# One output tensor with rows by partitions, nine unread products at the start, and an order for the first stage's splits in a hybrid encoder layer

## The chip, the cores and the metric

The kernel runs on one core of a Trainium2 chip. A core has a matrix engine (TensorE, PE in the profile, whose weight loads are shown apart as PEld), VectorE (DVE), ScalarE (ACT), GpSimd (POOL) and SyncE (SP), each with its own queue of instructions, and sixteen DMA engines that move data between main memory and the core. The metric is the device time of one execution in microseconds, lower is better; the time of a kernel is the median over its runs.

## The reference

One layer of a streaming encoder with two parallel mixers (a pooling mixer and a Mamba-2 scan, SSD) and a convolutional feed-forward block, for a prompt of 256 tokens and a sample of 32 tokens that share the weights. The width is 2048, the mixers have 1024 and 2048 channels, the feed-forward block 5632. Cut to what matters:

```
xn   = rmsnorm(x, norm_mix_pre)
proj = xn @ w_in                  # u | z | xBC | dt
y_pool, new_pool = pool_mixer(u, ...)
y_ssd, new_sconv, new_h = ssd_mixer(z, xbc, dt_raw, ...)
mix  = concat([y_pool, y_ssd]) @ w_out
x    = x + rmsnorm(mix, norm_mix_post)
hn   = rmsnorm(x, norm_ffn_pre)
up   = hn @ w_up
up, new_fconv = causal_dwconv(up, hist_fconv, ...)
f    = (silu(gate) * val) @ w_down
x    = x + rmsnorm(f, norm_ffn_post)
return x_prompt, x_sample, and the new states
```

All is float32. `rmsnorm` divides a token by the root of the mean of its squares over the 2048 channels.

## The kernel before

**Layout and products.** Channels lie on the 128 partitions, the 288 tokens (256 of the prompt, 32 of the sample) along the free axis, so x is sixteen tiles of 128 x 288, one for each k-step of a projection over 2048 channels. A float32 product is made of three products of a shorter format: each operand is split into a high part and a low part, and `mm3` (L135 to L138) adds weights-high by activations-high (L136), weights-high by activations-low (L137) and weights-low by activations-high (L138) in one PSUM accumulator. Plain float32 products occur too: the sum of squares (L242), the small projection for dt (L289) and some others.

**Weights.** They stream in through SP's queue into four buffers `raw`. ACT copies the high part, `whi` (L130, in the first stage L270), and DVE subtracts it from the original to get the low part, `wlo` (L131, L271), into four buffers each. A buffer comes free when TensorE has used it. In the same way ACT (L99) and DVE (L100) split the activations `xn`.

**The first stage** (L245 to L280) projects x onto six blocks of 128 columns (512 of the B and C inputs of the scan, 256 of its first channels): sixteen k-steps, 18 products each, in five accumulators `acc` and one `acc_x`. x is multiplied by the norm's gain but not yet by its reciprocal root: that, `rstd`, is applied when the accumulators are read out (L326, L327). Beside the splits, ACT squares the tiles of x (L230, L233; two buffers `xsq`), POOL adds the squares (L234), and at k = 13 `input_rstd` (L240) sums them over the channels by a product with `mean`, a tile filled with 1/2048 (`prs`, L242), followed by ACT's square root and DVE's reciprocal (L237, L238). After the stage come the products `pdt` (L289) and `pv` (L293) of the dt projection.

**The middle.** The projections of the mixers, the scan in groups of heads (decays `g`, masks `m`, products `py`), the output projection, the up projection and the down projection follow, each a call of `project`.

**The end.** Finished channel tiles are turned into rows of tokens by way of main memory (`fd`, `ft`). When the norm's factor of a row block is known, `y_out` (L963) multiplies and adds on DVE (L971) and writes 128 rows by 512 columns (256 KB) from SP's queue (L974). The second half of the prompt goes first, four writes; then the 32 sample rows, which lie as four blocks of 32 partitions (`xr_s`, 128 x 512), by one write (L1044); then the first half of the prompt, four writes.

**What sets the order.** Instructions are placed on each engine's queue by a scheduler from the program's order and priorities. `tc.keep_in_program_order` pins an instruction where the code has it, and `tc.issue_after(ins)` makes one stand behind another on the same engine. An engine works off its queue strictly from the front.

Of the kernel before, what the change touches and what calls it, by code (L numbers as in the profile page):

```python
# [8 lines left out]
F32 = mybir.dt.float32  # L9
F32R = mybir.dt.float32r  # L10
AF = mybir.ActivationFunctionType
# [5 lines left out]
P = 128  # L17
TC = {"schedule_with_timeline_sim": True}
D_MODEL = 2048
NP_ = 256  # L20
NS = 32
NT = NP_ + NS
D_POOL = 1024
D_SSD = 2048
# [6 lines left out]
NF = D_FF // P  # L31
NXC = CONV // P
NU = D_POOL // P
# [10 lines left out]
def body(  # L44
# [14 lines left out]
    w_up2,  # L59
    w_up,  # L60
    w_down,
    y_prompt,
    y_sample,
    new_pool,
    new_sconv,
    new_ssd_p,
# [4 lines left out]
    act, dve, pool, pe, sp = nc.scalar, nc.vector, nc.gpsimd, nc.tensor, nc.sync  # L71
# [11 lines left out]
    def aux(shape, name):  # L83
        return aux_ps.tile(shape, F32, tag="aux", name=name)

    def atile(name):
        return apool.tile([P, 2, NT], F32R, tag="a", name=name)
# [4 lines left out]
    def split_from(a, src, scale=None):  # L92

        if scale is None:
            act.activation(a[:, 0, :], src, AF.Copy)
            dve.tensor_tensor(a[:, 1, :], src, a[:, 0, :].bitcast(F32), op=ALU.subtract)
        else:
            return (
                act.activation(a[:, 0, :], src, AF.Copy, scale=scale),  # L99
                dve.scalar_tensor_tensor(  # L100
                    a[:, 1, :], src, scale, a[:, 0, :].bitcast(F32), op0=ALU.mult, op1=ALU.subtract
                ),
            )

    def wtile(part, n, nc_):

        t = wpool.tile([P, 1024 + 64], F32R, tag=part, name="w" + part)
        return t[:, 58 : 58 + n * nc_].rearrange("p (k c) -> p k c", k=n)
# [60 lines left out]
    def blocks_out(d, t, src, pool_):  # L169
# [12 lines left out]
    mean = const.tile([P, P], F32, name="mean")  # L182
# [4 lines left out]
        out=tri, in_=tri, pattern=[[1, P]], compare_op=ALU.is_ge, fill=0.0, base=0, channel_multiplier=-1  # L187
# [24 lines left out]
    g_mix_pre = const.tile([P, KD], F32, name="g0")  # L212
# [5 lines left out]
    start = ExitStack()  # L218
    xin = start.enter_context(tc.tile_pool(name="xin", bufs=1))
    xT = xin.tile([P, KD, NT], F32, name="xT")  # L220
# [4 lines left out]
    def input_tiles(kb, n):  # L225
        sp.dma_start(out=xT[:, kb : kb + n, :], in_=x_in[:, kb : kb + n, :])

    def input_squares(k):
        if k == 0:
            act.activation(xsum, xT[:, k, :], AF.Square)  # L230
        else:
            q = xin.tile([P, NT], F32, tag="xsq", bufs=2, name="xsq")
            act.activation(q, xT[:, k, :], AF.Square)  # L233
            pool.tensor_tensor(xsum, xsum, q, op=ALU.add)  # L234

# [4 lines left out]
    def input_rstd():  # L240
        p_ = aux([P, NT], "prs")
        pe.matmul(p_, mean, xsum, start=True, stop=True)  # L242
        root(rstd, p_)

    act.dma_start(out=g_mix_pre, in_=g0_in)  # L245
    input_tiles(0, 1)
    first = [acc_ps.tile([P, NT], F32, tag="acc", name="acc") if m < 5 else aux([P, NT], "acc_x") for m in range(6)]
    chunks = ((0, 1), (1, 1)) + tuple((k, 2) for k in range(2, KD, 2))
    x_with = {0: (1, 1), 1: (2, 2), 2: (4, 2), 4: (6, 3), 6: (9, 3), 8: (12, 4)}
    for kb, n in chunks:  # L250
        raw = wpool.tile([P, n, 768], F32, tag="raw", name="raw")
        sp.dma_start(out=raw, in_=w_first[:, kb : kb + n, :])
        if kb in x_with:
            input_tiles(*x_with[kb])
        if kb == 1:
            pool.dma_start(out=wdt, in_=w_dt)
        if kb == 2:
            pool.dma_start(out=par1, in_=par1_in)
            pool.dma_start(out=hp, in_=hp_in)
        if kb == 6:  # L260
            pool.dma_start(out=pc, in_=par2_in[:, :120])
            pool.dma_start(out=pf, in_=par2_in[:, 120:].rearrange("p (r t) -> p r t", r=6))
        for k in range(kb, kb + n):
            a = atile("xn")
            split_from(a, xT[:, k, :], g_mix_pre[:, k : k + 1])
            xn.append(a)
            hi, lo = wtile("hi", 1, 768)[:, 0, :], wtile("lo", 1, 768)[:, 0, :]
            step = 256 if k == 0 else 768
            for c in range(0, 768, step):
                act.activation(hi[:, c : c + step], raw[:, k - kb, c : c + step], AF.Copy)  # L270
                dve.tensor_tensor(  # L271
                    lo[:, c : c + step], raw[:, k - kb, c : c + step], hi[:, c : c + step].bitcast(F32), op=ALU.subtract
                )
            for t in range(k - 1, k) if 0 < k < 9 else range(2 * k - 10, 2 * k - 8) if 8 < k < 13 else ():
                input_squares(t)
            if k == 13:
                input_rstd()
            for m in range(6):
                c = slice(m * P, (m + 1) * P)
                mm3(first[m], hi[:, c], lo[:, c], a, k == 0, k == KD - 1)  # L280
# [5 lines left out]
    for r in range(4):  # L286
        for q in range(4):
            k = 4 * q + r
# [66 lines left out]
    def htile(name, n=NT, tag=None):  # L355
        return mp.tile([HEADS, n], F32, tag=tag or name, name=name, bufs={"z": 4}.get(tag, 2) if tag else 1)
# [22 lines left out]
    r = htile("r", tag="z")  # L379
# [196 lines left out]
    xT = op_.tile([P, KD, NT], F32, name="xT2")  # L576
# [66 lines left out]
    for t in range(NX):  # L643
        a = atile("mixs")
# [29 lines left out]
    for gi in range(2):  # L674
        c = slice(gi * P, (gi + 1) * P)
# [96 lines left out]
    for k in range(KD):  # L772
        if k % 2 == 0:
            raw = wpool.tile([P, 2, 896], F32, tag="raw", name="raw")
            with tc.high_priority(offset=ahead[0]):
                sp.dma_start(out=raw, in_=w_up1[:, k : k + 2, :])
        a = atile("hn")
        hi = act.activation(a[:, 0, :], x1[k], AF.Copy, scale=g_ffn_pre[:, k : k + 1])  # L778
# [8 lines left out]
        else:  # L787
            q = out_temp()
# [11 lines left out]
        for m in range(7):  # L800
            c = slice(m * P, (m + 1) * P)
# [32 lines left out]
    f = []  # L834
# [54 lines left out]
    for q in range(4):  # L889
        for b in range(2):  # L890
            t = apool.tile([P, 512], F32, tag="a", name="xr")
            sp.dma_start(out=t, in_=x1d[b * P : (b + 1) * P, 512 * q : 512 * (q + 1)])
            xr.append(t)
    xr_s = apool.tile([P, 512], F32, tag="a", name="xr_s")
# [68 lines left out]
    def y_out(q, b):  # L963

        x = xr[2 * q + b]
        f_ = ft[2 * q + b]
        for o, n, src in (
            ((0, 512, f_),) if q < 3 else ((0, 2 * P, f_[:, : 2 * P]), (2 * P, 2 * P, last[b]))
        ):
            c = slice(o, o + n)  # L970
            ins = dve.scalar_tensor_tensor(x[:, c], src, rf[:, b : b + 1], x[:, c], op0=ALU.mult, op1=ALU.add)  # L971
            if b:
                tc.keep_in_program_order(ins)
        sp.dma_start(out=y_prompt[0][b * P : (b + 1) * P, 512 * q : 512 * (q + 1)], in_=x)  # L974

    n_tok = [0]

# [20 lines left out]
    for kb, n in ((0, K_RUN), (K_RUN, 8), (K_RUN + 8, 8)):  # L998
        raw = fetch_w(wd2, kb, n, (KD - 2) * P, 256)
# [3 lines left out]
        for piece in split_w(raw, kb, n, 256):  # L1003
            for low in (True, False) if kb else (True,):
                for j in range(2):
                    c = slice(j * P, (j + 1) * P)
                    for k, hi, lo in piece:
                        a = f2[k]
# [8 lines left out]
    for j in range(2):  # L1017
        t = KD - 2 + j
# [4 lines left out]
    for j in range(2):  # L1023
        c = slice(j * P, (j + 1) * P)
# [16 lines left out]
    tc.keep_in_program_order(  # L1041
        dve.scalar_tensor_tensor(xr_s, ft_s, rf[:, 2:3], xr_s, op0=ALU.mult, op1=ALU.add)
    )
    sp.dma_start(out=y_sample[0].rearrange("s (q c) -> q s c", q=4), in_=xr_s)  # L1044
    p_f.append(acc_ps.tile([P, 4], F32, tag="acc", name="psum_f"))
    last[0] = acc_ps.tile([P, 2 * P], F32, tag="acc", name="pft")
    feature_sums(fsum, 1, True, False)
# [5 lines left out]
    for q in range(4):  # L1053
        y_out(q, 0)
# [1 line left out]


_OUTS = [
    (1, 256, 2048), (1, 32, 2048), (P, 2, 15, NU), (P, 2, 3, NXC), (P, D_SSD), (P, D_SSD), (P, 2, 2, 2 * NF),
]  # L1060


# [70 lines left out]
```

## Time and profile before

| | |
|---|---|
| median of 3 runs | 1330.14 us (1330.11 to 1331.14) |
| profiled execution | 1329.91 us |
| its span | 1328.2 us |
| TensorE busy | 1310.4 us (99%) |
| DVE, ACT, POOL busy | 884.6, 666.3, 215.0 us |
| moved by DMA | 249.81 MB, 188 GB/s on average |
| first product of the first stage | 5.71 us after the span's start |
| product `prs` (sum of squares) | 40.65 us |
| product `pdt` (after the first stage) | 48.32 us |
| last result row done by DVE | 1322.11 us |

The profile is one execution, recorded by the hardware. Its span is what lies between the first and the last instruction, and the execution took 1.71 us more. In a timeline a row has its start, its duration, the engine, the line and the operation with output and inputs; rows of one kind are folded (x3), and brackets hold the idle time of the engine ahead of it and what ended it. SPq rows are DMA issues. The matrix engine works in a pipeline, so that the duration of a product (0.3 us) is longer than the distance to the next (0.13 us).

### The profile page before, as it was taken

Reading aid. Unit: us, or ns where it says so; the run is one execution under the profiler, and the core shown is the slowest. Engines: PE = TensorE matmul, PEld = TensorE weight load, DVE = VectorE, ACT = ScalarE, POOL = GpSimd, SP = SyncE. Lnnn points to the kernel's source line nnn. Section 1 sums busy time; section 2 is a strip of 40 time slices with the busy share of each in tenths; the row PEclk is TensorE's granted clock in tenths of the full one; section 3 lists DMA queues with packets and bytes.
Section 4 is the critical chain, followed back from the end, with each engine's and each line's share of the span. In section 5 each row is a group of like instructions: output and inputs, shape, how many; then the busy total and the mean of one; then the engine's idle time right before and its main releaser. Section 6 shows DMA issues by size and latency. Waiting matters only on the chain.

```text
span 1328.2 us, 25077 instructions
## 1 busy us (share of the span) xinstructions
PE 1310.4 (99%) x10041; PEld 1295.1 (98%) x10041; DVE 884.6 (67%) x1460; ACT 666.3 (50%) x1002; POOL 215.0 (16%) x353
## 2 busy tenths in 40 slices
PE   7999999999999999999999999999999999999997
PEld 7999999999999989999999999999999999999996
DVE  8898998779644478977666643345666666664444
ACT  7558777446443455645445443334444444454442
POOL 6221102121211100211111100001111111101110
PEclk9999999999999999999999999999999999999998
DMA  7668884465666445666454454455444544566663
GB/s 287 230 194 255 287 242 160 140 240 206 232 206 207 147 143 195 199 188 185 164 183 162 151 175 161 160 180 177 172 159 164 186 159 159 175 235 175 209 181 93
DMA packets 104008, 249.81 MB, mean 188 GB/s; under 512 B 63748, under 2 KB 69444, under 8 KB 81492
## 3 DMA queue, kind: packets, MB, share of 16 engines
q1 hardware_dynamic: 101972, 243.11, 55.8%
q0 software_dynamic: 1488, 4.92, 1.1%
q8 instruction: 78, 1.28, 0.4%
q14 instruction: 38, 0.31, 0.1%
q10 hardware_dynamic: 432, 0.19, 0.1%
HBM read 236.23 MB, written 11.95 MB: 187 GB/s over the span
## 4 chain that ended last, share of the span: by engine, by line
PE 98%; DVE 1%; DMA 0%; ACT 0%; issue 0%; DVEq 0%; SPq 0%
PE acc L138 31%; PE acc L136 31%; PE acc L137 31%; PE acc_x L138 1%; PE acc_x L137 1%; PE acc_x L136 1%; PE py L467 1%; DVE xr L971 0%; PE run_a L1014 0%; PE low L1012 0%; DMA raw<-in_w_first 0%; PE py L469 0%; PE pst L701 0%; PE run_b L1027 0%; PE pdt L289 0%; DVE mg L764 0%
## 5 line engine op out<-in xcount | busy, mean ns | idle before, releaser
L131 DVE TENSOR_TENSOR wlo<-raw,whi 128x1024 fp32r<-128x1024 f32 (+1 forms) x386 | 464.0, 1203 | 334.7 <-ACT whi L130 332.5
L130 ACT ACTIVATE whi<-raw 128x1024 fp32r<-128x1024 f32 (+1 forms) x386 | 399.6, 1037 | 474.5 <-PE acc L137 382.9
L136 PE MATMUL acc<-hn,whi 128*128 128x288 f32 x1360 | 399.0, 294 | 0.1
L137 PE MATMUL acc<-hn,whi 128*128 128x288 f32 x1360 | 398.1, 293 | 0.0
L138 PE MATMUL acc<-hn,wlo 128*128 128x288 f32 x1360 | 397.7, 293 | 0.0
L136 PEld LDWEIGHTS acc<-hn,whi 128*128 128x128 f32 x1360 | 255.3, 188 | 0.9 <-ACT hn L778 0.9
L137 PEld LDWEIGHTS acc<-hn,whi 128*128 128x128 f32 x1360 | 255.3, 188 | 0.1
L138 PEld LDWEIGHTS acc<-hn,wlo 128*128 128x128 f32 x1360 | 255.2, 188 | 0.0
L136 PE MATMUL acc<-xn,whi 128*128 128x288 f32 x688 | 203.6, 297 | 5.7 <-ACT whi L270 5.7
L137 PE MATMUL acc<-xn,whi 128*128 128x288 f32 x688 | 200.6, 293 | 0.0
L138 PE MATMUL acc<-xn,wlo 128*128 128x288 f32 x688 | 198.6, 298 | 1.3 <-DVE wlo L271 1.3
L136 PE MATMUL acc<-fa,whi 128*128 128x288 f32 x660 | 194.0, 294 | 0.0
L137 PE MATMUL acc<-fa,whi 128*128 128x288 f32 x660 | 193.4, 293 | 0.0
L138 PE MATMUL acc<-fa,wlo 128*128 128x288 f32 x660 | 193.1, 293 | 0.0
L136 PEld LDWEIGHTS acc<-xn,whi 128*128 128x128 f32 x688 | 130.2, 189 | 6.6 <-ACT whi L270 5.7
L137 PEld LDWEIGHTS acc<-xn,whi 128*128 128x128 f32 x688 | 130.1, 189 | 0.2
L138 PEld LDWEIGHTS acc<-xn,wlo 128*128 128x128 f32 x688 | 127.8, 189 | 2.1 <-DVE wlo L271 1.5
L136 PEld LDWEIGHTS acc<-fa,whi 128*128 128x128 f32 x660 | 124.1, 188 | 0.0
L138 PEld LDWEIGHTS acc<-fa,wlo 128*128 128x128 f32 x660 | 123.9, 188 | 0.0
L137 PEld LDWEIGHTS acc<-fa,whi 128*128 128x128 f32 x660 | 123.9, 188 | 0.0
L825 POOL COPY fc_stage<-ebuf 128x4 f32<-128x4 f32 x88 | 27.2, 310 | 501.2 <-DVE ebuf L824 501.2
L831 DVE SCALAR_TENSOR_TENSOR fc<-ebuf,pf,fc 128x290 f32<-128x290 f32 x176 | 90.2, 518 | 2.9 <-ACT fc L829 0.3
(277 smaller groups left out, 1692.0 us busy)
## 6 DMA issues: line engine op xcount, KB each, us to landing
raw<-in_w_up SPq DMA_DIRECT2D x80, 1024.0 KB, 4.8
raw<-in_w_in SPq DMA_DIRECT2D x38, 1024.0 KB, 5.4
raw<-in_w_down SPq DMA_DIRECT2D x32, 1024.0 KB, 4.8
raw<-in_w_out SPq DMA_DIRECT2D x24, 1024.0 KB, 4.9
raw<-in_w_down SPq DMA_DIRECT2D x16, 768.0 KB, 4.3
raw<-in_w_up SPq DMA_DIRECT2D x8, 896.0 KB, 4.6
gb<-g_d SPq DMA_DIRECT2D x8, 832.0 KB, 6.4
raw<-in_w_first SPq DMA_DIRECT2D x7, 768.0 KB, 10.1
```

The lines of the kernel that those rows point to most:

```text
L130: act.activation(hi, raw[:, k : k + n, :], AF.Copy)
L131: dve.tensor_tensor(lo, raw[:, k : k + n, :], hi.bitcast(F32), op=ALU.subtract)
L136: pe.matmul(out, wh, a[:, 0, :], start=start, stop=False)
L137: pe.matmul(out, wh, a[:, 1, :], start=False, stop=False)
L138: pe.matmul(out, wl, a[:, 0, :], start=False, stop=stop)
L467: pe.matmul(y[:, 0:256], xw[:, 0, c], m[:, j, 0:256], start=True, stop=False)
L825: pool.tensor_copy(fc_stage[:, :, :, i], e[:, 256:324].rearrange("p (s c) -> p s c", c=34)[:, :, 0:2])
L831: dve.scalar_tensor_tensor(c, e[:, r_ : r_ + 290], pf[:, r_, i : i + 1], c, op0=ALU.mult, op1=ALU.add)
```

## The change

Three edits.

1. The two outputs `y_prompt` (1 x 256 x 2048) and `y_sample` (1 x 32 x 2048) become one, `y_rows` (128 x 9 x 512): for each partition eight pieces of prompt rows and one of sample rows. The host puts them back in shape.
2. Nine products of `mean` with itself, whose result `idle` nothing reads, stand at the front of TensorE's queue.
3. In the first stage the activation splits of step k stand behind the weight splits of step k - 2, and the squares behind the high split of step k - 1; squares have four buffers instead of two; `input_rstd` comes at k = 14 instead of 13.

```diff
-            q = xin.tile([P, NT], F32, tag="xsq", bufs=2, name="xsq")
+            q = xin.tile([P, NT], F32, tag="xsq", bufs=4, name="xsq")
...
+    cut = []
+    idle = aux([P, P], "idle")
+    for i in range(9):
+        tc.keep_in_program_order(pe.matmul(idle, mean, mean, start=True, stop=True))
...
             a = atile("xn")
-            split_from(a, xT[:, k, :], g_mix_pre[:, k : k + 1])
+            with ExitStack() as order:
+                for ins in cut[k - 2] if k > 2 else ():
+                    order.enter_context(tc.issue_after(ins.ins))
+                split_from(a, xT[:, k, :], g_mix_pre[:, k : k + 1])
...
-                act.activation(hi[:, c : c + step], raw[:, k - kb, c : c + step], AF.Copy)
-                dve.tensor_tensor(
+                w_hi = act.activation(hi[:, c : c + step], raw[:, k - kb, c : c + step], AF.Copy)
+                w_lo = dve.tensor_tensor(
...
+            cut.append((w_hi, w_lo))
             for t in range(k - 1, k) if 0 < k < 9 else range(2 * k - 10, 2 * k - 8) if 8 < k < 13 else ():
-                input_squares(t)
-            if k == 13:
+                with tc.issue_after(cut[k - 1][0].ins):
+                    input_squares(t)
+            if k == 14:
                 input_rstd()
...
-        sp.dma_start(out=y_prompt[0][b * P : (b + 1) * P, 512 * q : 512 * (q + 1)], in_=x)
+        sp.dma_start(out=y_rows[:, 4 * b + q, :], in_=x)
...
-    sp.dma_start(out=y_sample[0].rearrange("s (q c) -> q s c", q=4), in_=xr_s)
+    sp.dma_start(out=y_rows[:, 8, :], in_=xr_s)
...
 _OUTS = [
-    (1, 256, 2048), (1, 32, 2048), (P, 2, 15, NU), (P, 2, 3, NXC), (P, D_SSD), (P, D_SSD), (P, 2, 2, 2 * NF),
+    (P, 9, 512), (P, 2, 15, NU), (P, 2, 3, NXC), (P, D_SSD), (P, D_SSD), (P, 2, 2, 2 * NF),
 ]
...
+    y_p = _np.ascontiguousarray(y[:, :8].reshape(P, 2, D_MODEL).transpose(1, 0, 2)).reshape(1, NP_, D_MODEL)
+    y_s = _np.ascontiguousarray(y[:, 8].reshape(4, NS, 512).transpose(1, 0, 2)).reshape(1, NS, D_MODEL)
```

How the queues change is best seen in their order. First DVE in the first stage, from the third k-step on: `xn` are activation splits, `wlo` weight splits, `rstd` the reciprocal. Before:

```order
L100 SCALAR_TENSOR_TENSOR xn<-xT,g_125,xn 128x288 x2
L271 TENSOR_TENSOR wlo<-raw,whi 128x768 x2
L100 SCALAR_TENSOR_TENSOR xn<-xT,g_125,xn 128x288 x6
L271 TENSOR_TENSOR wlo<-raw,whi 128x768 x2
L100 SCALAR_TENSOR_TENSOR xn<-xT,g_125,xn 128x288 x4
L271 TENSOR_TENSOR wlo<-raw,whi 128x768 x8
L131 TENSOR_TENSOR wlo<-raw,whi 128x1024
L238 RECIPROCAL rstd<-rstd 128x288
```

Now, up to the same end (ahead of these rows, two activation splits and two weight splits alternate from k = 4 on):

```order
L99 SCALAR_TENSOR_TENSOR xn<-xT,g_125,xn 128x288 x2
L277 TENSOR_TENSOR wlo<-raw,whi 128x768 x2
L99 SCALAR_TENSOR_TENSOR xn<-xT,g_125,xn 128x288 x2
L277 TENSOR_TENSOR wlo<-raw,whi 128x768
L99 SCALAR_TENSOR_TENSOR xn<-xT,g_125,xn 128x288
L277 TENSOR_TENSOR wlo<-raw,whi 128x768
L99 SCALAR_TENSOR_TENSOR xn<-xT,g_125,xn 128x288
L277 TENSOR_TENSOR wlo<-raw,whi 128x768 x2
L130 TENSOR_TENSOR wlo<-raw,whi 128x1024 x2
L237 RECIPROCAL rstd<-rstd 128x288
```

Where six and then four activation splits stood together, none stands more than two ahead of a weight split. Two weight splits of the next projection, not one, stand ahead of the reciprocal.

TensorE at the start of its queue, now (before, it begins with the second of these rows; rows that repeat are left out):

```order
L249 MATMUL idle<-mean 128x128 x9
L135 MATMUL acc<-xn,whi 128x288
L136 MATMUL acc<-xn,whi 128x288
L137 MATMUL acc<-xn,wlo 128x288 x2
L135 MATMUL acc_x<-xn,whi 128x288
```

The product `prs` stands behind 252 products of the stage where it stood behind 234.

SP's queue around the decays `g`, whose rows go to main memory and come back as `gb`. Before:

```order
L175 DMA xs_d<-blocks 32x9x32
L392 DMA g_d<-g 32x416
L175 DMA xs_d<-blocks 32x9x32 x3
L437 DMA gb<-g_d 128x1664 x2
L441 DMA xw<-xs_d 128x2x256
```

Now:

```order
L400 DMA g_d<-g 32x416
L174 DMA xs_d<-blocks 32x9x32 x4
L445 DMA gb<-g_d 128x1664 x2
L449 DMA xw<-xs_d 128x2x256
L450 DMA xw<-xs_d 128x256
```

The write of g has moved ahead of the first of the four writes of `xs_d`. On DVE and ACT there are more small moves of this kind up to about 250 us of the program, mostly weight splits that stand one place earlier among the vector work. At the end of SP's queue only a form changes: the write of `xr_s` is `4x32x512` before and `128x512` now.

More of the change, by code (lines that the diff above doesn't have):

```diff
@@ L61, in body @@
     w_down,
-    y_prompt,
-    y_sample,
+    y_rows,
     new_pool,
@@ L1119 @@
     r = _run(nc, [arrays], core_ids=[0])
-    y_p, y_s, n_pool, n_sconv, h_p, h_s, n_fconv = (_np.asarray(r.results[0][f"out_{i}"]) for i in range(len(_OUTS)))
+    y, n_pool, n_sconv, h_p, h_s, n_fconv = (_np.asarray(r.results[0][f"out_{i}"]) for i in range(len(_OUTS)))
     def rows(a, s):
```

## The prediction

> **What bounds the kernel now.** I read the page first, then TensorE's waits, then the timeline of the two ends of the span, since a kernel whose TensorE hardly pauses can gain only where it does.
>
> ```profile
> span 1328.2 us, 25077 instructions
> PE 1310.4 (99%) x10041; PEld 1295.1 (98%) x10041; DVE 884.6 (67%) x1460; ACT 666.3 (50%) x1002; POOL 215.0 (16%) x353
> PE 98%; DVE 1%; DMA 0%; ACT 0%; issue 0%; DVEq 0%; SPq 0%
> PE acc L136 <- ACT whi L270: 5.7, 1, 5.7
> PE acc L138 <- DVE wlo L271: 1.3, 1, 1.3
> ```
>
> The first rows are the span and each engine's busy time, the third the chain of work that ended last, the last two are TensorE's longest waits (total, times, longest). The span is 1328.2 us, TensorE is busy for 1310.4 of it, and 98% of the chain runs on it. So the kernel is a queue of products, and there are four places to gain: the 5.7 us before the first product, products that run slowly, the one wait of 1.3 us, and what follows the last product. The change touches all of these. The profiled execution took 1329.91 us, 1.71 more than its span and 0.23 less than the median, 1330.14; I sum against 1329.91 and add the 0.23 at the end.
>
> **The nine products ahead.** The timeline of the start (start, duration, engine, line, operation, and in brackets what ended the idle time before):
>
> ```profile
> 0.95 0.20 POOL L183 MEMSET mean<- 128x128 f32 x1
> 5.71 0.61 PE L136 MATMUL acc<-xn,whi 128*128 128x288 f32 x1 [5.71 <-ACT whi L270]
> 6.36 0.44 PE L136 MATMUL acc<-xn,whi 128*128 128x288 f32 x1
> 6.60 0.44 PE L137 MATMUL acc<-xn,whi 128*128 128x288 f32 x1
> 10.42 1.58 ACT L270 ACTIVATE whi<-raw 128x768 fp32r<-128x768 f32 x2 [1.47 <-DMA raw<-in_w_first]
> 11.14 0.29 PE L137 MATMUL acc<-xn,whi 128*128 128x288 f32 x1
> 11.27 0.30 PE L136 MATMUL acc<-xn,whi 128*128 128x288 f32 x1
> 12.86 0.29 PE L136 MATMUL acc<-xn,whi 128*128 128x288 f32 x1
> ```
>
> Products start 0.24 us apart at 6.36 and 6.60 and 0.13 apart at 11.14 and 11.27: TensorE starts at about half its rate. The step lies between 10.7 and 10.9, 5.1 us after the first product. The clock column says 1.00 in this stretch, so the pitch is my evidence. These windows count what ran slowly:
>
> ```profile
> 5.71:10.80 5.09, 5.09 (x21) 5.09 (x22) 3.95 (x7) 3.62 (x9) 2.49 (x5) 1.00 1.01 375
> 10.80:12.86 2.06, 2.06 (x17) 2.06 (x16) 1.57 (x3) 2.00 (x4) 0.00 (x0) 1.00 1.03 416
> 12.86:48.32 35.46, 34.16 (x257) 33.66 (x255) 30.22 (x33) 23.67 (x44) 15.65 (x19) 1.00 0.74 279
> ```
>
> Twenty-one products at 0.24 cost 21 x 0.11 = 2.3 us more than fast ones. Not all can be had. The k-step that starts at 12.86 is the third one (k = 2); its weights are split by the ACT row at 10.42, whose two pieces take 0.79 each, so whi is there at 11.21, and that row itself waited for the transfer. Before that moment products of k = 2 cannot run at any clock. With a fast clock from the start, 36 products take 36 x 0.1325 = 4.8 us and end at 10.5; TensorE then waits for 11.21. So the third k-step starts near 11.25 instead of 12.86: **-1.6 us**.
>
> Are the nine done by 5.71? They read mean alone, written by 1.15. Their price comes from the one fp32 product of similar kind:
>
> ```profile
> 40.65 0.65 PE L242 MATMUL prs<-xsum,mean 128*128 128x288 f32 x2
> 40.81 0.48 PE prs L242 x2
> ```
>
> The first is the product's two records in the timeline, the second its share in the chain: 0.48 us for 288 columns, so 0.21 for 128, and about 0.43 at the slow pitch. Nine take 1.9 to 3.9 us and end between 3.2 and 5.2, ahead of 5.71. If the clock steps 5.1 us after the first of them, that is at 6.4. A step up to about 7.3 costs nothing (seven slow products lose 0.8 us, what lies between 10.5 and 11.25). The bounds: no effect on the clock, 0; step before 7.3, -1.6. I take the upper end, because in this trace steady products did release the clock after 5.1 us and the nine start 4.4 us earlier.
>
> The Trainium skill, TensorE: Matmul & The Clock Gate, Part 1: The HAM clock gate, says the rate is released after a busy window of about 3.4 us whose phase is free-running. By it the step would fall 3.4 to 6.8 us after the first of the nine, at 4.7 to 8.1, and the term would be -1.25 to -1.6; the trace's 5.1 us lies inside.
>
> **The order of the splits in the first stage.** DVE writes the low parts of activations (L100) and weights (L271) in one queue:
>
> ```profile
> 17.98 4.32 DVE L100 SCALAR_TENSOR_TENSOR xn<-xT,g,xn 128x288 fp32r<-128x288 f32 x6
> 25.19 3.53 DVE L100 SCALAR_TENSOR_TENSOR xn<-xT,g,xn 128x288 fp32r<-128x288 f32 x4
> 28.64 5.63 DVE L271 TENSOR_TENSOR wlo<-raw,whi 128x768 fp32r<-128x768 f32 x5
> 28.65 0.30 PE L137 MATMUL acc_x<-xn,whi 128*128 128x288 f32 x1
> 30.25 0.94 PE L138 MATMUL acc<-xn,wlo 128*128 128x288 f32 x5 [1.30 <-DVE wlo L271]
> ```
>
> Six and then four activation splits stand ahead of weight splits that TensorE needs sooner. Its product at 28.65 is followed at 30.25 instead of 28.78: 1.46 us lost from start to start (1.30 in the wait's own count). The new order has pairs: two activation splits, two weight splits. A pair of each costs 2 x 0.72 + 2 x 0.75 = 2.9 us on DVE against 4.8 us for two k-steps on TensorE (18 products of 0.1325 each), so DVE stays ahead. The transfers fill 0.74 of the stretch from 12.86 to 48.32 (the third window above), and no wait of TensorE in it is put down to one, so I take it that they land in time when needed 3 us earlier; ACT's splits stand in the same pairs. **-1.46 us**, bounds -1.3 and -1.46, and 0 if a piece is still late.
>
> A check: from 11.25, fourteen k-steps of 2.385 and the 0.48 of the sum of squares end at 45.1. Before, the product after them started here:
>
> ```profile
> 48.32 2.15 PE L289 MATMUL pdt<-xT,wdt 128*32 128x288 f32 x32
> 43.62 1.96 DVE L238 RECIPROCAL rstd<-rstd 128x288 f32<-128x288 f32 x1 [0.59 <-ACT rstd L237]
> ```
>
> That is 3.1 us earlier, as the two terms say.
>
> **The sum of squares one k-step later, four buffers for squares.** The reciprocal ended 45.58 - 40.65 = 4.9 us after its product began. Moved one k-step (2.4 us) later, it ends about 0.3 us before the stage's last product (36 products, 4.8 us, and its own 0.48 lie between), and the five accumulators are multiplied by it while TensorE does pdt (2.15 us). The group of the first evacuations by DVE:
>
> ```profile
> L326 DVE TENSOR_TENSOR ebuf<-acc,rstd 128x256 f32<-128x256 f32 x5 | 2.1, 419 | 0.3 <-POOL ebuf L319 0.3
> ```
>
> Behind the reciprocal stand one weight split (1.2 us), two of these (0.42 each) and a small rest (0.2, an estimate by its 32 columns), so the first accumulator is free about 1.9 us after the stage's end and needed 2.2 after it: a cover of 0.3. If it failed, TensorE would wait for DVE's next evacuations, up to 1 us. I take 0 and keep +1.
>
> **The output tensor.** The tail, on SP's queue and DVE:
>
> ```profile
> 1315.26 2.45 SPq L974 DMA_DIRECT2D out<-xr  x4
> 1318.62 0.70 SPq L1044 DMA_DIRECT2D out<-xr_s  x1
> 1320.02 4.14 SPq L974 DMA_DIRECT2D out<-xr  x4
> 1321.63 0.48 DVE L971 SCALAR_TENSOR_TENSOR xr<-pft,rf,xr 128x256 f32<-128x256 f32 x1
> DMA to landing us min/median/max: 2.0/2.1/2.1
> L974 SPq DMA_DIRECT2D out<-xr x2: 391/812/1233, 1322.4 to 1322.9; - x2
> DMA to landing us min/median/max: 4.2/4.2/4.3
> 1320.00:1321.00 1.00, 0.00 (x0) 0.00 (x0) 1.00 (x2) 0.00 (x0) 0.00 (x0) 1.00 0.32 25
> 1323.00:1324.00 1.00, 0.00 (x0) 0.00 (x0) 0.00 (x0) 0.00 (x0) 0.00 (x0) 0.50 0.93 350
> ```
>
> The four writes ahead of the sample's issue quickly and land 2.0 to 2.1 us after issue (first landing row). The four behind take 4.14 us to issue, and the last two, issued at 1322.4 and 1322.9, land 4.2 to 4.3 after. In between the queues move 25 GB/s, later 350 (last column): the sample write, which goes out as 4 x 32 x 512, trickles and holds those behind it. In the new kernel it is 128 x 512, the same form as its neighbours, so I give it and the last four the 2.1 us of the first four. DVE finishes the last xr at 1321.63 + 0.48 = 1322.11; its write lands at 1324.25 where the last one landed at 1322.9 + 4.3 = 1327.2. **-2.95 us**; bounds 0 (the trickle has another cause) and -3.0.
>
> The Trainium skill, DMA: Bandwidth & Descriptors, Why a DMA increments its semaphore by 16 and not by 1, says that a transfer runs on the largest number of engines up to 16 that divides the slowest dimension on both sides: 4 for the old form, 16 for the new. It would give the same term; the windows' 25 GB/s against 350 agree with it.
>
> One tensor fewer and the reshaping on the host lie outside the span's work: 0, since 1.71 us around the span show no room for more than a few tenths.
>
> **What moves afterwards.** Up to about 250 us DVE, ACT and SP run in a slightly different order, and everything starts 3 us earlier. TensorE waits nowhere there now, but the margins are thin:
>
> ```profile
> 129.78 1.89 DVE L460 TENSOR_TENSOR m<-m,cbt 128x1664 f32<-128x1664 f32 x1
> 131.76 0.65 PE L467 MATMUL py<-m,xw 128*64 128x256 f32 x4
> 178.50 1.22 DVE L131 TENSOR_TENSOR wlo<-raw,whi 128x1024 fp32r<-128x1024 f32 x1
> 180.07 0.29 PE L138 MATMUL acc<-xn,wlo 128*128 128x288 f32 x1
> ```
>
> The mask product is done at 131.67 and read at 131.76, 0.1 us later; a weight split is done at 179.72 and read at 180.07, 0.35 later. Were the vector work not to move earlier with TensorE, up to 3.0 us of the gain would come back as waits there. It should move: the splits between 50 and 95 us wait for TensorE's release of their buffers, the weight splits stand a place earlier in the new order, and the transfer of the decays (g) is issued sooner. I take +0.3, bounds 0 and +3.0.
>
> **Sum:** -1.6 - 1.46 - 2.95 + 0.3 = -5.71, or 1324.20 on the profiled execution, **1324.4 us** beside the median.
>
> **Rivals.** (a) The sample write was not what held the tail, for instance because DVE's late rows or the closing clock do. For it: the clock column stands at 0.50 in the last of those windows. Against it: DVE is done at 1322.11 and data flows for 4 us more. Only -2.76 remains: 1327.4. Chance 0.10. (b) Waits after 100 us take back the stage's gain, because SSD transfers rather than TensorE set the pace; for it speaks the 0.1 us margin: 1329.91 - 2.95 + 0.23 = 1327.2. Chance 0.10. (c) The clock is not released by unread products or comes late: without the -1.6, 1326.0. Chance 0.07. (d) Slower: the nine do not overlap their weight loads and run one record after the other at the slow rate. By the cold rows a record would be 0.33 load and 0.44 product, two records each, p = 1.54 a product. They end at 1.3 + 9p = 15.2; the weights have landed meanwhile, the stage then takes 38.7 us and ends at 53.9 instead of 48.3. Less the tail's 2.95 that is +2.65: 1332.8. It is slower than before from p = 1.25 on. Against it: in the trace a weight load runs while the product before it does:
>
> ```profile
> 5.88 0.33 PEld L137 LDWEIGHTS acc<-xn,whi 128*128 128x128 f32 x1
> ```
>
> It lies inside the product of 5.71 to 6.32. Chance 0.05. The Trainium skill speaks for (d): TensorE: Matmul & The Clock Gate, What overlaps and what doesn't, lets a weight load overlap only where the row groups differ, which here they don't; the row disagrees. (e) The change does not act: the unread products are not run, or two rivals fall together, (a) with (b) giving no change. Chance 0.06, half of it slower than before.
>
> **Numbers.** The forecast holds 0.62: its own range is 1323.5 (every term at its best, with 0.3 for the scatter of runs) to 1325.5. To leave out no more than 0.2 the range goes to 1327.4, which takes in (c), (b) and half of (a). About 0.2% (2.7 us, 1327.5 and 1332.8) is what a measurement here can tell from no change. Faster: 0.62 + 0.07 and most of (a) and (b), 0.82; same 0.10, from the far halves of (a) and (b) and part of (e); slower 0.08, from (d) and (e).
>
> **What would show it.** The clock: products 0.13 apart soon after 6.4, the third k-step at 11.25; 0.24 beyond 8 would speak for (c). The first real product still at 5.71; at 10 or later, (d). The 1.3 us row of TensorE's waits gone and pdt at 45.2; a new row on wlo, or on acc against DVE's evacuations, says which term failed. The last four writes issued in some 0.35 us each and landing 2.1 after; the span ending 2.2 to 3 us after DVE's last row rather than 6.1; otherwise (a). Waits of TensorE on m, ce or wlo between 100 and 210 us would be (b). Wrong in kind I would be if TensorE's busy time fell or grew by more than 3 us in a stretch that I have not named.

## The result: 1324.07 us, and the profile after

| | before | changed |
|---|---|---|
| median of 5 runs | 1330.12 us (1330.04 to 1331.14) | 1324.07 us (1323.57 to 1324.38) |
| ratio, with its 95% interval | | 0.9951 [0.9938, 0.9964] |
| profiled execution | 1329.91 us | 1323.83 us |
| its span | 1328.2 us | 1322.1 us |

The changed kernel is 6.05 us faster by the medians; the forecast was 1324.4. The page after, with the rows that answer to the first ones of before:

```profile
span 1322.1 us, 25117 instructions
PE 1312.0 (99%) x10059; PEld 1296.7 (98%) x10059; DVE 882.6 (67%) x1460; ACT 667.1 (50%) x1002; POOL 224.9 (17%) x353
```

TensorE's waits (total, times, longest), whole list:

```profile
PE idle L249 <- POOL mean L182: 1.2, 1, 1.2
PE acc L135 <- ACT whi L276: 1.2, 1, 1.2
PE psum_f L939 <- ACT fsq L968: 0.8, 1, 0.8
PE psum_m L753 <- ACT msq L676: 0.7, 1, 0.7
```

The wait on a low weight split is gone. In its place stands one of 1.2 us on a high split (ACT's), which was not there. The first row is no loss: it is what comes ahead of the nine products. The timeline shows where the second one lies:

```profile
1.21 4.04 PE L249 MATMUL idle<-mean 128*128 128x128 f32 x18 [1.21 <-POOL mean L182]
5.32 0.40 PE L135 MATMUL acc<-xn,whi 128*128 128x288 f32 x1
5.56 0.30 PE L136 MATMUL acc<-xn,whi 128*128 128x288 f32 x1
10.67 1.58 ACT L276 ACTIVATE whi<-raw 128x768 fp32r<-128x768 f32 x2 [1.25 <-DMA raw<-in_w_first]
11.57 0.40 PE L135 MATMUL acc<-xn,whi 128*128 128x288 f32 x1 [1.18 <-ACT whi L276]
45.65 2.15 PE L297 MATMUL pdt<-xT,wdt 128*32 128x288 f32 x32
```

The nine products (18 records) run from 1.21 to 5.25, done before the first real one. That one starts at 5.32 and the pitch is fast almost at once. But at 11.57, where the third k-step starts, TensorE has stood still for 1.18 us: ACT's split began at 10.67, when the transfer of these weights had landed. The product after the stage starts at 45.65 instead of 48.32.

The tail:

```profile
1315.61 0.33 SPq L1052 DMA_DIRECT2D out<-xr_s  x1
1317.01 2.45 SPq L982 DMA_DIRECT2D out<-xr  x4
1318.62 0.48 DVE L979 SCALAR_TENSOR_TENSOR xr<-pft,rf,xr 128x256 f32<-128x256 f32 x1
DMA to landing us min/median/max: 2.0/2.0/2.1
1319.00:1320.00 1.00, 0.00 (x0) 0.00 (x0) 0.10 (x1) 0.00 (x0) 0.00 (x0) 0.53 0.98 363
```

All eight writes of result rows land 2.0 to 2.1 us after issue (fourth row), the four behind the sample's write issue as fast as those ahead of it (2.45 us for four, 4.14 before), and in the microsecond from 1319 us on, in which DVE finishes its last row (1319.10), the queues already move 363 GB/s.

The account between the two profiled executions, by four marks:

| stretch | before | changed | difference | forecast |
|---|---|---|---|---|
| span's start to the third k-step | 12.86 | 11.57 | -1.29 | -1.6 |
| third k-step to `pdt` | 35.46 | 34.08 | -1.38 | -1.46 |
| `pdt` to DVE's last result row | 1273.79 | 1273.45 | -0.34 | +0.3 |
| that row to the span's end | 6.09 | 3.00 | -3.09 | -2.95 |
| sum | 1328.2 | 1322.1 | -6.1 | -5.71 |

The sizes stand close to the forecast's. Whether the causes are those of the forecast was the question of the experiments.

### The profile page after: what moved, and what is told of

Its sections match the earlier page's. It is cut to its first block, busy times and chain, and to the rows that moved or that the text cites. A ratio compares the mean times of both kernels' runs of the same rounds, so it can differ in the third digit from the quotient of the medians.

```text
span 1322.1 us, 25117 instructions
## 1 busy us (share of the span) xinstructions
PE 1312.0 (99%) x10059; PEld 1296.7 (98%) x10059; DVE 882.6 (67%) x1460; ACT 667.1 (50%) x1002; POOL 224.9 (17%) x353
## 4 chain that ended last, share of the span: by engine, by line
PE 98%; DVE 1%; DMA 1%; ACT 0%; SPq 0%; issue 0%; DVEq 0%
PE acc L135 31%; PE acc L137 31%; PE acc L136 31%; PE acc_x L137 1%; PE py L475 1%; PE acc_x L135 1%; PE acc_x L136 1%; DMA raw<-in_w_first 1%; DVE xr L979 0%; PE run_a L1022 0%; PE low L1020 0%; PE py L477 0%; PE pst L709 0%; PE run_b L1035 0%; PE pdt L297 0%; DVE mg L772 0%
## 5 line engine op out<-in xcount | busy, mean ns | idle before, releaser
L137 PE MATMUL acc<-xn,wlo 128*128 128x288 f32 x688 | 194.9, 295 | 0.0
L829 POOL COPY ebuf<-pf 128x2 f32<-128x2 f32 x88 | 71.2, 810 | 122.8 <-DVE fc L839 79.4
```

Source lines behind the costliest of these rows:

```text
L137: pe.matmul(out, wl, a[:, 0, :], start=False, stop=stop)
L829: pool.tensor_copy(e[:, 258:260], pf[:, 4:6, i])
```

## The experiments

In all of them the kernel before was run beside on the same chip; its medians lay between 1329.94 and 1330.49 us. The ratios are to it.

**One: the output tensor alone.** The edit to the kernel before, beside the host's reshaping:

```diff
-        sp.dma_start(out=y_prompt[0][b * P : (b + 1) * P, 512 * q : 512 * (q + 1)], in_=x)
+        sp.dma_start(out=y_rows[:, 4 * b + q, :], in_=x)
...
-    sp.dma_start(out=y_sample[0].rearrange("s (q c) -> q s c", q=4), in_=xr_s)
+    sp.dma_start(out=y_rows[:, 8, :], in_=xr_s)
```

> The kernel before with the one output tensor alone. My theory: the sample write in the form 128 x 512 no longer holds the four writes behind it, so the span ends about 3.0 us after DVE's last result row instead of 6.1, and nothing else moves: 1327.0 to 1327.2 us. Rival: the three gains of the change are not independent, and the tail gains only because the tail runs at another moment or clock: 1329 or more.

Measured: 1327.76 us, ratio 0.9979 [0.9970, 0.9988]. The profiled execution gave 1326.76. The gain is 2.7 us, and TensorE's wait of 1.3 us on the low split is still in its list. The median lies 0.6 us above the range expected, the profiled execution 0.2 below it; the span ends 3.07 us after DVE's last row, as expected. The tail is a term of its own.

**Two: the form without the one tensor.** Two output tensors, the sample's as 128 x 512:

```diff
-    sp.dma_start(out=y_sample[0].rearrange("s (q c) -> q s c", q=4), in_=xr_s)
+    sp.dma_start(out=y_sample, in_=xr_s)
...
-    (1, 256, 2048), (1, 32, 2048), ...
+    (1, 256, 2048), (P, 512), ...
```

> The kernel before with its two output tensors kept, but the sample's laid out as 128 x 512, so that its write goes out in that form. If the form of the one write is what held the tail, the last four writes land 2.1 us after issue and the gain is that of the one tensor, 2.7 to 3.1 us. If one tensor for all rows matters, the time stays that of the kernel before.

Measured: 1327.10 us, ratio 0.9978 [0.9969, 0.9986]. Issues of SP at the end, and the landing of the last four writes:

```profile
1318.59 0.33 SPq L1044 DMA_DIRECT2D out<-xr_s  x1
1319.99 2.45 SPq L974 DMA_DIRECT2D out<-xr  x4
DMA to landing us min/median/max: 2.0/2.1/2.2
```

The whole of the tail's gain is there with two tensors. It is the form of one write of 256 KB, not the number of tensors.

**Three: the nine products alone.**

```diff
+    idle = aux([P, P], "idle")
+    for i in range(9):
+        tc.keep_in_program_order(pe.matmul(idle, mean, mean, start=True, stop=True))
```

> The kernel before with the nine unread products alone. Theory A: DVE's queue in the first stage has no idle time from 11.3 to 34.3 us, so the weight split that TensorE waits for still ends at 30.2; the third k-step starts 1.3 us earlier, the wait at that split grows from 1.3 to about 2.6 us, and the time stays at 1330.1 (1329.8 to 1330.3). Theory B, as the sum of the prediction has it: the terms add, and the time is 1328.6 to 1328.9.

Measured: 1331.12 us, beside 1330.49 for the kernel before, ratio 1.0006 [0.9997, 1.0014]: nothing gained. That is 0.8 us above theory A's range, on the far side from theory B. TensorE in the first stage:

```profile
11.71 0.40 PE L136 MATMUL acc<-xn,whi 128*128 128x288 f32 x1 [1.13 <-ACT whi L273]
22.66 0.40 PE L136 MATMUL acc<-xn,whi 128*128 128x288 f32 x1 [1.11 <-ACT whi L273]
30.65 0.93 PE L138 MATMUL acc<-xn,wlo 128*128 128x288 f32 x5 [1.36 <-DVE wlo L274]
48.74 1.66 PE L292 MATMUL pdt<-xT,wdt 128*32 128x288 f32 x24
```

The third k-step starts 1.15 us earlier than in the kernel before (11.71 against 12.86), TensorE then waits 1.11 us more for a high split and again for the low one, and `pdt` comes no earlier (48.74 against 48.32). Theory A stands, with one difference: what was gained is lost at a second wait, not by a longer first one. That second wait is for ACT: its high split starts at 21.78, behind a square that stood 0.54 us waiting for POOL's sum. The terms of the forecast do not add.

**Four: the changed kernel without the nine products.**

```diff
-    idle = aux([P, P], "idle")
-    for i in range(9):
-        tc.keep_in_program_order(pe.matmul(idle, mean, mean, start=True, stop=True))
```

> The changed kernel without the nine unread products. The start falls back to the slow pitch, 0.24 us between products until about 10.8 us, and the third k-step to 12.9 us: 1.3 us more than the changed kernel, 1325.2 to 1325.5. If the clock rose for another reason than the nine products, it stays at 1324.1.

Measured: 1324.14 us (1323.86 to 1324.58), ratio 0.9953 [0.9940, 0.9965], against 1324.07 with them. The number is the one of the second expectation, but not for its reason: the slow pitch did come back, as the first had it, and the time did not.

```profile
5.34 0.61 PE L135 MATMUL acc<-xn,whi 128*128 128x288 f32 x1 [5.34 <-ACT whi L273]
5.98 0.44 PE L135 MATMUL acc<-xn,whi 128*128 128x288 f32 x1
6.22 0.44 PE L136 MATMUL acc<-xn,whi 128*128 128x288 f32 x1
...
8.86 0.59 PE L137 MATMUL acc<-xn,wlo 128*128 128x288 f32 x3
9.29 0.30 PE L137 MATMUL acc_x<-xn,wlo 128*128 128x288 f32 x1
9.43 0.29 PE L135 MATMUL acc<-xn,whi 128*128 128x288 f32 x1
...
11.81 0.30 PE L135 MATMUL acc<-xn,whi 128*128 128x288 f32 x1
...
45.68 2.15 PE L294 MATMUL pdt<-xT,wdt 128*32 128x288 f32 x32
```

Products are 0.24 us apart at 6 us, and the three from 8.86 to 9.29 take 0.14 each: here the fast pitch begins 3.5 us after the first product (8.86 against 5.34), not 5.1. Even with about 15 slow products the third k-step starts at 11.81, 0.24 later than with the nine, because with them TensorE waits there for the transfer. From there to `pdt` are 33.87 us, which is exactly fourteen k-steps of 2.385 and the 0.48 of `prs`: no wait.

**Five: the order alone**, without the nine products and with two output tensors:

```diff
-            split_from(a, xT[:, k, :], g_mix_pre[:, k : k + 1])
+            with ExitStack() as order:
+                for ins in cut[k - 2] if k > 2 else ():
+                    order.enter_context(tc.issue_after(ins.ins))
+                split_from(a, xT[:, k, :], g_mix_pre[:, k : k + 1])
...
-            q = xin.tile([P, NT], F32, tag="xsq", bufs=2, name="xsq")
+            q = xin.tile([P, NT], F32, tag="xsq", bufs=4, name="xsq")
...
-                input_squares(t)
-            if k == 13:
+                with tc.issue_after(cut[k - 1][0].ins):
+                    input_squares(t)
+            if k == 14:
```

> The kernel before with the order of the splits, the four buffers and the later sum of squares alone (no unread products, two output tensors). Both theories: the wait of 1.3 us on the weight split is gone and the first product after the stage starts at 46.9 instead of 48.3. The further 0.3 us at the second group of masked products (131.8 us) also goes if the order of DVE's queue made it, and stays if only the moment did: 1328.4 or 1328.7 us.

Measured: 1327.17 us, ratio 0.9975 [0.9966, 0.9985]. Both theories missed the time by more than a microsecond. `pdt` starts at 45.95, a microsecond earlier than they had it: the fast pitch began 4.0 us after the first product in this execution instead of 5.1, and the third k-step stands at 12.09 instead of 12.86. By the medians the order alone is worth 3.3 us (2.7 between the profiled executions); with the tail's 2.7 this makes 6.05, as much as the whole change gained. The second group of masked products starts 0.23 us after the product ahead of it (0.42 before); its mask is done 1.6 us ahead. In the kernel before, the group starts at 131.76, and this is the product ahead of it:

```profile
131.34 0.29 PE L138 MATMUL acc<-xn,wlo 128*128 128x288 f32 x1
```

In the profiles with the old order this distance is 0.42, 0.64, 0.22 and 0.23 (before, and experiments three, one and two): with the old order it differed from profile to profile. No profile with the whole new order shows the wait.

**Six and seven: the order in halves.** The first piece of that diff alone (the activation splits), and the other two alone (the squares, and `prs` one k-step later).

> The kernel before with the order of the activation splits alone (squares in two buffers and in their old places, sum of squares at k = 13). If the pairs on DVE's queue are what removed the wait, TensorE has no wait on a weight split and the first product after the stage stands at 45.9 to 46.8 as with the whole order: 1327.1 to 1328.4 us. If the squares' two buffers hold ACT, and by it DVE, part of the wait stays.

> The kernel before with the other half: four buffers and bound places for the squares, the sum of squares one k-step later, the activation splits in their old order. By the same reason the wait on the weight split stays at 1.3 us or near it and the time at that of the kernel before, 1329.6 to 1330.3 us. If ACT's waits for the squares were the cause, the wait goes.

Measured: 1328.41 us, ratio 0.9985 [0.9976, 0.9994], and 1327.41 us, ratio 0.9976 [0.9967, 0.9985]. The first has no wait on a weight split, as expected, but `pdt` stands at 47.20 instead of 45.9 to 46.8, since the slow pitch lasted longest in this profile (the rows are shown further down). The second expectation missed: with six and four activation splits still ahead of the weight splits, the wait on the low split is gone as well. So the order of the splits was enough to remove the wait, but it was not its only cause. The trace of the first half shows the other one. DVE and POOL:

```profile
18.01 0.93 DVE L100 SCALAR_TENSOR_TENSOR xn<-xT,g,xn 128x288 fp32r<-128x288 f32 x2
18.95 3.48 POOL L234 TENSOR_TENSOR xsum<-xsum,xsq 128x288 f32<-128x288 f32 x4
23.93 2.81 POOL L234 TENSOR_TENSOR xsum<-xsum,xsq 128x288 f32<-128x288 f32 x3 [1.50 <-ACT xsq L233]
24.04 2.04 DVE L100 SCALAR_TENSOR_TENSOR xn<-xT,g,xn 128x288 fp32r<-128x288 f32 x2
```

Two splits of activations take 0.93 us at 18.0, ahead of POOL's sums, and 2.04 us at 24.0, beside them.

**Eight: the kernel before with POOL's sums left out.** All tiles of x between the first and the last are left out of the sum of squares:

```diff
-            pool.tensor_tensor(xsum, xsum, q, op=ALU.add)
+            if k == KD - 1:
+                pool.tensor_tensor(xsum, xsum, q, op=ALU.add)
```

> The kernel before, with the sums of the squares of all tiles of x but the first and the last left out (POOL adds one tile instead of fifteen; ACT still squares them). The order of DVE's splits is that of before, six and four activation splits together. If DVE's splits are slow there because POOL's adds run at the same time, an activation split takes about 0.5 us instead of 0.7 to 1.0 and a weight split 0.95 instead of 1.2 to 1.5 all through, the wait of 1.3 us on the weight split is gone, and the time is 1327.4 to 1328.6 us. If the order alone is the cause, the wait stays at 1.0 us or more and the time at 1329.7 to 1330.3.

Measured: 1327.50 us, ratio 0.9984 [0.9975, 0.9993]. DVE's activation splits between 11 and 30 us, in the kernel before, in the one with the squares' half alone, and in this one, all three with the same order on DVE's queue:

```profile
L100 DVE SCALAR_TENSOR_TENSOR xn<-xT,g,xn 128x288 fp32r<-128x288 f32 x12 | 9.9, 883 | 0.0
```

```profile
L100 DVE SCALAR_TENSOR_TENSOR xn<-xT,g,xn 128x288 fp32r<-128x288 f32 x12 | 8.2, 736 | 0.0
```

```profile
L100 DVE SCALAR_TENSOR_TENSOR xn<-xT,g,xn 128x288 fp32r<-128x288 f32 x12 | 5.6, 513 | 0.5 <-ACT xn L99 0.5
```

The columns behind the bar are busy time in all and nanoseconds of one; neighbouring splits overlap a little, so that the first is less than twelve times the second. Twelve splits take 9.9, 8.2 and 5.6 us, the weight splits 1294, 1221 and 1010 ns each, and TensorE's wait on the low split is there in the first kernel only. POOL's sums cost DVE its lead. Each of these rows has its waits in the last column, apart from the durations, so that a DVE that waits less for ACT does not explain the shorter splits. The new order does not make the activation splits faster: in the changed kernel, in the same stretch, one takes 887 ns. The order only puts them behind weight splits that TensorE needs sooner:

```profile
L277 DVE TENSOR_TENSOR wlo<-raw,whi 128x768 fp32r<-128x768 f32 x10 | 11.0, 1136 | 2.3 <-ACT whi L276 2.2
L99 DVE SCALAR_TENSOR_TENSOR xn<-xT,g,xn 128x288 fp32r<-128x288 f32 x8 | 6.9, 887 | 0.1
```

**Nine to eleven: the landing.** In the changed kernel the third k-step waits for weights. The first of three kernels fetches them singly; the second also moves POOL's early transfers back; the third is the second without the nine products. (`adds` holds POOL's sums; the transfer of x that stood behind the third k-step's weights now stands behind the fourth's; the product of `wdt` with the gain moves behind DVE's twelfth low split.)

```diff
-    chunks = ((0, 1), (1, 1)) + tuple((k, 2) for k in range(2, KD, 2))
+    chunks = tuple((k, 1) for k in range(4)) + tuple((k, 2) for k in range(4, KD, 2))
...
-        sp.dma_start(out=raw, in_=w_first[:, kb : kb + n, :])
+        got = sp.dma_start(out=raw, in_=w_first[:, kb : kb + n, :])
         if kb in x_with:
-            input_tiles(*x_with[kb])
+            with tc.issue_after(got.ins):
+                input_tiles(*x_with[kb])
...
-        if kb == 1:
-            pool.dma_start(out=wdt, in_=w_dt)
...
         if kb == 6:
-            pool.dma_start(out=pc, in_=par2_in[:, :120])
-            pool.dma_start(out=pf, in_=par2_in[:, 120:].rearrange("p (r t) -> p r t", r=6))
+            with tc.issue_after(adds[-1].ins):
+                pool.dma_start(out=wdt, in_=w_dt)
+                pool.dma_start(out=pc, in_=par2_in[:, :120])
+                pool.dma_start(out=pf, in_=par2_in[:, 120:].rearrange("p (r t) -> p r t", r=6))
```

> The changed kernel with the weights of the third and fourth k-step fetched one by one instead of as a pair, each x transfer pinned behind the weights it followed in the code. If the landing of the weights bounds the start, the wait of 1.2 us ahead of the third k-step falls to 0.3 or less and the first product after the stage moves from 45.65 to about 44.6, unless the pair behind (k = 4 and 5, there at 14.9) is late next, which would leave 0.3 to 0.6 of the gain: 1323.0 to 1323.8 us. If something else holds the third k-step, 1324.1.

> The same, and three transfers of POOL's queue (the small weights of dt, and parameters of later stages, 0.6 MB in all) moved from 4 us to behind the first squares' sums, so that they do not share the DMA engines with the first weights. If landings bound the start, no wait is left in the stage: first product after the stage at 44.4, 1322.7 to 1323.1 us. If the early transfers cost nothing: as the run without this edit.

> The same without the nine unread products. With landings out of the way the slow pitch at the start shows: 15 to 24 products at 0.24 instead of 0.13, 1.6 to 2.5 us, less what waits are left: 0.9 to 1.6 us slower than with them. If unread products are worth nothing at any landing, the two are equal.

Measured: 1323.08 us (1322.79 to 1323.43), ratio 0.9948 [0.9936, 0.9961]; 1322.60 us (1322.17 to 1322.77), ratio 0.9944 [0.9931, 0.9956]; 1324.01 us (1323.45 to 1324.81), ratio 0.9955 [0.9941, 0.9969]. The first and the third lie where they were expected, the second 0.1 us below its range. Single fetches leave 0.7 us of waits in the stage, moving POOL's transfers takes these away, and now the nine products are worth 1.4 us, with no overlap between the runs with and without them. The third k-step and `pdt`, with them and without:

```profile
10.91 0.29 PE L135 MATMUL acc<-xn,whi 128*128 128x288 f32 x1
...
44.67 2.15 PE L299 MATMUL pdt<-xT,wdt 128*32 128x288 f32 x32
```

```profile
12.68 0.30 PE L135 MATMUL acc<-xn,whi 128*128 128x288 f32 x1
...
46.37 2.15 PE L296 MATMUL pdt<-xT,wdt 128*32 128x288 f32 x32
```

In the first of these two profiles the slow pitch goes on after the nine products:

```profile
1.20 4.21 PE L249 MATMUL idle<-mean 128*128 128x128 f32 x18 [1.20 <-POOL mean L182]
6.60 0.35 PE L135 MATMUL acc<-xn,whi 128*128 128x288 f32 x1
6.79 0.30 PE L136 MATMUL acc<-xn,whi 128*128 128x288 f32 x1
```

Here a record still takes 0.44 us at 6.36, and the fast pitch begins at 6.79, 5.6 us after the first of the nine. In the changed kernel's profile the rate rises among the nine: their last two records, from 4.78 on, take 0.35 and 0.27 us where the ones ahead take 0.42, 3.6 to 3.8 us after the first of the nine.

The kernel with both edits and the nine, at 1322.60 us, lies 1.5 us below the changed one (1324.07). The two were not run side by side: the kernel before stood at 1330.12 beside the one and at 1329.94 beside the other.

## Why the prediction was right in the time, and where it was wrong in the cause

**The tail: right, in cause and size.** It was sized at -2.95 and measured -3.09 in the profile; alone it gave 2.7 to 2.8 us by the medians. The form of the sample's write is the cause, by experiment two. Rival (a) is out.

**The nine products: the step failed.** The prediction took -1.6 us for them and added it to the rest. They do what the text said of the clock, and sooner: the rate rises at about 4.9, where it counted with 6.4, they end at 5.25, ahead of the first real product, and that one is followed at the fast pitch within 0.3 us. But alone they gain nothing, and beside the order of the splits they gain 0.07 us, which these runs cannot tell from nothing. Two things were overlooked in the sum. First, in the kernel before a faster TensorE only runs into a late ACT and then into DVE's queue, which has no pause from 11.3 us to the split that TensorE waits for, so the term could not be had without the other. This is the whole list of DVE's waits in the kernel before from 8 to 34 us; the longer of the two ends at 11.29, the other one lies ahead of it:

```profile
DVE wlo L271 <- ACT whi L270: 1.6, 2, 1.1
```

The prediction worked each term out as if the other were done. Second, the comparison point was one execution's clock. In the profile before, the rate rose 5.1 us after the first product; without the nine it rose 3.5 us after it in experiment four, and later than either in the first half of the order:

```profile
5.75 0.61 PE L136 MATMUL acc<-xn,whi 128*128 128x288 f32 x1 [5.75 <-ACT whi L274]
11.44 0.44 PE L137 MATMUL acc<-xn,whi 128*128 128x288 f32 x1
11.90 0.30 PE L137 MATMUL acc<-xn,whi 128*128 128x288 f32 x1
12.04 0.29 PE L136 MATMUL acc<-xn,whi 128*128 128x288 f32 x1
```

Between 11.44 and 11.90 lie two products at about 0.23, and from there the pitch is 0.14: 6.1 us after the first. With a step at 3.5 us the third k-step starts at 11.81, and the landing of its weights forbids anything before 11.5 (ACT's split begins at 10.67 and takes 0.79 for the first piece). The room for the nine products is then a quarter of a microsecond; with the step at 6.1 it is nearly two (the third k-step at 13.36 in experiment six). The gate, the split of the third k-step's weights, was named in the prediction by its start at 10.42; it came at 10.67, and the third k-step 0.3 us later than forecast (11.57 against 11.25).

**The wait on the low split: right in size, half right in cause.** -1.46 was forecast and -1.38 measured. The prediction blamed the six and four activation splits ahead of the weight splits. Pairing them does remove the wait (experiment six), but so does moving the squares with the queue's order left alone (seven), or leaving the sums out (eight). What made DVE late was the queue's order together with POOL: beside POOL's sums an activation split took 883 ns where it takes 513 without. The quoted rows had it in them: six splits in 4.32 us and four in 3.53, 0.72 and 0.88 each, where a row of the start shows 0.52 for one:

```profile
3.93 0.52 DVE L100 SCALAR_TENSOR_TENSOR xn<-xT,g,xn 128x288 fp32r<-128x288 f32 x1 [1.87 <-ACT xn L99]
```

One price of this step was wrong: the forecast put a weight split at 0.75 us, where its own quoted row has five in 5.63, 1.13 each, and the changed kernel shows 1.14. Two splits of each kind are then 4.05 us (0.887 and 1.136 each) and not 2.9, against TensorE's 4.8 for two k-steps. DVE stays ahead all the same, with less than half of the lead that was forecast.

On what POOL's sums do to the splits, the Trainium skill, SBUF — State Buffer, Who interferes with whom, has the rule: a VectorE instruction with two inputs in SBUF and a GpSimd instruction that reads SBUF use one read port and shut each other out. The splits are such instructions, and 513 against 883 ns agrees with it.

**What moves afterwards: wrong in sign, by 0.6 us.** +0.3 was allowed and -0.34 measured, and the price lies at the place that the prediction named as thin: the second group of masked products waited in the kernel before (0.42 us after the product ahead of it instead of 0.22) and does not any more, which is 0.20 of the 0.34. Its mask is ready earlier, at 125.96:

```profile
128.25 0.29 PE L137 MATMUL acc<-xn,wlo 128*128 128x288 f32 x1
128.47 0.65 PE L475 MATMUL py<-m,xw 128*64 128x256 f32 x4
```

The product and its successor are 0.22 apart. Where the other 0.14 comes from is not worked out. Rival (b), that waits give the stage's gain back, did not come true.

**The sum of squares one k-step later** cost nothing, as forecast: no wait of TensorE on an evacuation is in the list.

**The rivals.** (c) had the nine products without effect and the time at 1326.0; the effect was nil and the time 1324.1, because without them, in experiment four, the third k-step stands at 11.81 already, 1.05 us earlier than in the kernel before. The first product came 0.37 us earlier there (5.34 against 5.71) and the fast pitch 1.6 us sooner after it. That the pitch came so soon is chance, as far as these runs show, and five runs do not say how often a late one comes. (d) is out: the nine ran in 4.04 us, 0.45 each, as the prediction's slow price (0.43) had it. (e) is out too: the nine are in the timeline, and the time moved by 6.05 us.

So the right sum was made of one term that stood, one of right size with half its cause, and one that would have been had without its edit. That the time came out within 0.4 us of the forecast is in this last part luck. The profile after alone would not have told: its account by four marks agrees with the forecast to 0.7 us in every row. What stays open is how often an execution without the nine products meets a late step and would lose by it.

## What to carry to other kernels

Terms at one stage do not add when two engines take turns in being late: work out each edit with the others left out, and see which queue is late next. A warmed-up clock is worth only what the transfers leave: here nothing that could be measured with ACT's split of the third k-step starting at 10.67 us, and 1.4 us once it started at 9.17. An engine's row that is slower than the same row elsewhere in the trace (0.72 to 1.03 us against 0.5) is a lead of its own: look what the neighbour engine reads at that moment.

## What the runs showed of the hardware that was not expected

- The same split on DVE takes 513 ns with POOL's sums left out and 883 ns beside them, and the loss is not even: 0.93 or 2.04 us for two within one trace.
- The moment at which TensorE's rate rises moves from execution to execution: from 3.5 to 6.1 us after the first product in the nine profiles without unread products. In the four profiles that have them it came 2.8 to 5.6 us after the first of them (earliest in the kernel with single fetches, where the records shorten from 0.42 to 0.27 us between 3.9 and 4.1 us); the 2.8 lies outside the 3.4 to 6.8 us that the prediction quotes. A single profile's start is no measure of what a warm-up is worth.
- A write of 256 KB that goes out as 4 x 32 x 512 held the four writes behind it for 3 us; as 128 x 512 it issues in 0.33 us instead of 0.70 and holds nothing.
